# First stage: v of two heads and q, k of a third head in bursts over four k-tiles, summed in SBUF

## The chip, the core and the metric

The kernel runs on one core of one Trainium2 chip. The time is device microseconds of one launch. Engines are named as the profile names them: PE (TensorE matmul; PEld is its weight load), DVE (VectorE), ACT (ScalarE), POOL (GpSimd) and SP (SyncE, which issues most transfers).

## What is computed

One layer of a diffusion backbone (DEPTH is 1): 512 latent tokens and 256 context tokens, 2048 channels, 16 heads of 128, all in f32. A conditioning vector gives shifts, scales and gates by six 2048 x 2048 products (`ada`); then neighbourhood attention with context keys, its output projection, a LayerNorm, a SwiGLU FFN and a second LayerNorm. The part that the change touches is this:

```python
sh1, sc1, g1, sh2, sc2, g2 = [m[:, None, :] for m in ada_params(c, ada_w[i], ada_b[i])]
h = modulate(x, sh1, sc1)                     # x * (1 + sc1) + sh1
hc = modulate(xc, csh1, csc1)
q, k, v = [split_heads(t) for t in jnp.split(h @ w_qkv, 3, axis=-1)]
k_c, v_c = [split_heads(t) for t in jnp.split(hc @ w_qkv[:, D_MODEL:], 2, axis=-1)]
y = neighbourhood_attention(q, k, v, k_c, v_c, na_rpb[j]) @ na_w_o[j]
```

## The kernel before

Every f32 product is made of three `float32r` products (`mm3`: hi x hi, hi x lo, lo x hi). A weight or an activation is first split into hi and lo by `split`: a copy on ACT (line 77) and a subtraction on DVE (line 78). Line 81 is the one matmul call behind nearly all products, so rows are told apart by their tiles.

**First stage.** It walks over 16 k-tiles of 128 channels (`KT`). For k-tile kt, `ada_start` loads four 512 KB pieces of the modulation weights (`wr_an`) and multiplies them with `sil` into bank 7 (`adp`, 32 short matmul rows); `ada_cols` turns the result into the columns `md` of shift and scale; `h_start` loads 128 rows of x (`xr`, 256 KB) and of the context (`cr`, 128 KB) through POOL's queue, modulates them on DVE and splits them into the activations `a_h` and `hc`; `qkv_start` loads a 384 KB piece of `w0` and accumulates q and k of heads 0 and 1 (`acc`, 4 banks), v of both for the latent tokens (2 banks) and their context keys (1 bank). So seven banks are open for the whole stage and the eighth serves `adp`. `ada_start` runs one k-tile ahead of `qkv_start`. All raw pieces come from a ring of six buffers in pool `p0`; `xr` and `cr` share two buffers (`stg`), so the next `xr` is loaded only when the last one has been split.

**Between the stages.** `evac_q` and `split` empty the banks into q, k and v. Then pool `p0` is closed and the pools `pb` and `p1r` are opened in its place: `s_c` (the conditioning vector on all partitions, 1 MB, SiLU on ACT), `mask` and each head's bias table `br` (POOL's queue), and a ring of three raw buffers for weights.

**Attention stage.** `v_block(0, v0, [4, 5])` makes the context v of heads 0 and 1; then for each pair hp, `v_block` makes v of both heads, and `q_block`, `k_block` q and k of each head. The steps of a head's attention (`attn`: four scores with softmax, seven steps of transposition `tr` and product with v into `o`) are queued and interleaved with the blocks of the heads after it (`pop`); what is left is put in front of the next block by `flush`. `ada_more` puts the other modulation columns between the blocks: a load of two 512 KB pieces each (`wr_ada`) and two reductions on DVE (line 141). Each queue and engine works in the order in which a scheduler has written its instructions.

Of the kernel before, what the change touches and what calls it, by code (L numbers as in the profile page):

```python
# [9 lines left out]
F32 = mybir.dt.float32  # L10
F32R = mybir.dt.float32r
AF = mybir.ActivationFunctionType
ALU = mybir.AluOpType
# [4 lines left out]
P = 128  # L18
D = 2048
KT = D // P  # L20
T = 512
C = 256
# [11 lines left out]
U = 1024  # L34
# [9 lines left out]
def build(tc, ins, out):  # L44
    nc = tc.nc
    with ExitStack() as top:
# [5 lines left out]
        def bank(i, name):  # L52
            return psp.tile([P, T], F32, tag=f"b{i}", name=name)
# [11 lines left out]
        act_hi = [None] * KT  # L65
        act_lo = [None] * KT
# [86 lines left out]
        hc_hi = [hcx[k // 2][:, k % 2 * T:k % 2 * T + C] for k in range(KT)]  # L153
        hc_lo = [hcx[k // 2][:, k % 2 * T + C:k % 2 * T + T] for k in range(KT)]

        with ExitStack() as ph1:
            pa = ph1.enter_context(tc.tile_pool(name="pa", bufs=1))
# [4 lines left out]
            def new_q(h):  # L162
                return [pa.tile([P, T], F32R, tag=f"q{i}", name=f"q{h}_{i}", bufs=2) for i in "hl"]

            def new_k(h):
                return [pa.tile([P, T + C], F32R, tag=f"k{i}", name=f"k{h}_{i}", bufs=2) for i in "hl"]

            def new_v(hp):
                return [[pa.tile([P, 2 * P], F32R, tag=f"v{t}{i}", name=f"v{hp}_{t}{i}") for i in "hl"]
                        for t in range(6)]  # L170

            def evac_q(ps, q):
                nc.scalar.activation(q[0], ps, AF.Copy, scale=QSCALE)
                nc.vector.scalar_tensor_tensor(out=q[1], in0=ps, scalar=QSCALE, in1=q[0].bitcast(F32),
                                               op0=ALU.mult, op1=ALU.subtract)

            q0, q1, k0, k1, v0 = new_q(0), new_q(1), new_k(0), new_k(1), new_v(0)

            def half(b, x):
                return b[:, (x % 2) * 256:(x % 2) * 256 + 256]  # L180

            accs = [bank(i, f"acc{i}") for i in range(7)]
            rows, mods = {}, {}

            def ada_start(kt):
# [30 lines left out]
                split(hc_hi[kt], hc_lo[kt], cr[:, :C])  # L216

            def qkv_start(kt):
                wh, wl = unit(ins["w0"][kt], f"w0{kt}", 768)
# [6 lines left out]
                for t in range(4):  # L226
                    ts = slice(t * P, (t + 1) * P)
                    mm3(half(accs[4 + t // 2], t), act_hi[kt][:, ts], act_lo[kt][:, ts],
                        wh[:, 512:768], wl[:, 512:768], f and t % 2 == 0, l)
                for i in (1, 3):  # L230
                    sl = slice(i * P, (i + 1) * P)
                    mm3(half(accs[6], i // 2), wh[:, sl], wl[:, sl], hc_hi[kt], hc_lo[kt], f and i == 1, l)

            with tc.tile_pool(name="p0", bufs=6) as p0:
                rp[0] = p0
                sil = p0.tile([P, KT, 32], F32, name="sil", bufs=1)
                nc.gpsimd.memset(sil, 0.0)
                for i in range(2):
                    nc.vector.tensor_copy(sil[:, :, i], cv[:, i])
                ada_start(0)  # L240
                biases()
                ada_cols(0)
                for kt in range(KT):
                    h_start(kt)
                    if kt + 1 < KT:
                        ada_start(kt + 1)
                    qkv_start(kt)
            for i, (q, k) in enumerate(((q0, k0), (q1, k1))):
                evac_q(accs[2 * i], q)
                split(k[0][:, :T], k[1][:, :T], accs[2 * i + 1])  # L250
                split(k[0][:, T:], k[1][:, T:], half(accs[6], i))
            for t in range(4):
                split(v0[t][0], v0[t][1], half(accs[4 + t // 2], t))
# [169 lines left out]
            for hp in range(1, NH // 2):  # L423
                if hp == 1:
                    enqueue(attn(1, q1, k1, v0), 24)
                v = new_v(hp)
                v_block(hp, v, list(range(6)))
                flush()
                ada_more(3)
                for i in range(2):  # L430
                    h = hp * 2 + i
                    q, k = new_q(h), new_k(h)
                    q_block(h, q)
                    ada_more(1)
                    k_block(h, k)
# [679 lines left out]
def _lay(inp):  # L1115
    a = {k: np.asarray(v) for k, v in inp.items()}
    ct = np.ascontiguousarray
    r = {}
    x = a["x"].reshape(ROWS, NB, BAND, D).transpose(1, 0, 2, 3).reshape(T, D)
    r["xT"] = ct(x.T).reshape(KT, P, T)  # L1120
    r["ctxT"] = ct(a["ctx"].reshape(C, D).T).reshape(KT, P, C)
    r["c"] = ct(a["c"].reshape(D))
    r["cv"] = ct(np.stack([a["c"].reshape(KT, P).T, a["c_ctx"].reshape(KT, P).T], 1))
    aw = a["ada_w"][0]
    r["ada_n"] = ct(aw[:, :2 * D].reshape(KT, P, 2, KT, P).transpose(3, 1, 0, 2, 4)).reshape(KT, P, KT * 2 * P)
    r["ada_t"] = ct(aw[:, 2 * D:].T).reshape(64, P, D)
# [8 lines left out]
    r["w0"] = ct(np.concatenate([w[:, :, 0, 0], w[:, :, 1, 0], w[:, :, 0, 1], w[:, :, 1, 1],  # L1135
                                  w[:, :, 2, 0], w[:, :, 2, 1]], -1))
# [28 lines left out]
```

## Time and profile before

| | us |
|---|---|
| median of 3 runs | 2503.3 (2501.56 to 2512.56) |
| the profiled execution | 2513.77 |
| its span, first to last instruction | 2512.0 |
| PE busy | 2420.1 (96%) |
| DVE busy | 1836.1 (73%) |
| ACT busy | 1038.4 (41%) |
| mean granted TensorE clock | 0.994 |

Busy PE time is modelled: a matmul's row ends later than the next one starts, so work on PE is counted here from start to start. The first stage lies between 0 and 152.6 us of the span, the attention stage from there to about 1000 us.

### The profile page before, as it was taken

How to read it: one execution, taken by the hardware profiler on the slowest of the kernel's cores; microseconds unless marked ns; L12 is line 12 of the kernel's file. 1: busy time of each engine (PE TensorE's matmuls, PEld its weight loads, DVE VectorE, ACT ScalarE, POOL GpSimd, SP SyncE). 2: the span in 40 equal slices, each digit the busy share in tenths (PEclk: the TensorE clock that was granted, in tenths of full speed). 3: DMA queues.
4: the chain of work that ended last, by engine and by line, in shares of the span. 5: the costliest groups of instructions: out<-in, count | busy, mean ns of one | idle time of the engine just before them, and what ended most of it. 6: DMA issues, size and time to landing. Idle time of an engine off the chain costs nothing.

```text
span 2512.0 us, 45142 instructions
## 1 busy us (share of the span) xinstructions
PE 2420.1 (96%) x18588; PEld 2295.4 (91%) x18588; DVE 1836.1 (73%) x2619; ACT 1038.4 (41%) x1590; POOL 234.2 (9%) x348
## 2 busy tenths in 40 slices
PE   7889999999999999999999999999999989999997
PEld 5688989898998988999999999999999979999897
DVE  3365655565565567999888888878888887878978
ACT  2242322222232235548444444444444544645545
POOL 1110101000010000110110100101011000000021
PEclk9999999999999999999999999999999999999999
DMA  9964444444544453655443434433344565754685
GB/s 334 326 231 154 145 162 139 154 155 154 165 154 156 136 187 129 193 121 191 136 133 118 137 124 137 140 120 130 125 144 153 183 196 129 205 158 126 176 185 127
DMA packets 142543, 406.18 MB, mean 162 GB/s; under 512 B 16544, under 2 KB 40496, under 8 KB 142208
## 3 DMA queue, kind: packets, MB, share of 16 engines
q1 hardware_dynamic: 116608, 342.42, 41.5%
q0 software_dynamic: 25728, 60.88, 9.9%
q8 instruction: 145, 2.38, 0.4%
q14 instruction: 62, 0.51, 0.1%
HBM read 351.85 MB, written 40.89 MB: 156 GB/s over the span
## 4 chain that ended last, share of the span: by engine, by line
issue 38%; PE 35%; DMA 11%; DVE 9%; POOL 4%; ACT 2%; SPq 0%; POOLq 0%; ACTq 0%; DVEq 0%
DMA wr_ada<-ada_t 7%; PE qp L81 5%; PE kp L81 4%; PE vp L81 4%; PE cp L81 2%; PE g_1b L81 2%; POOL setT L594 2%; PE y L81 2%; DVE wr_ada L141 2%; PE g_5b L81 1%; PE g_4b L81 1%; PE g_3b L81 1%; PE g_2b L81 1%; PE g_0b L81 1%; POOL setB L594 1%
## 5 line engine op out<-in xcount | busy, mean ns | idle before, releaser
L623 DVE TENSOR_TENSOR wr_f<-wr_f,wr_f 128x1024 f32<-128x1024 f32 x164 | 199.9, 1219 | 3.1 <-DMA wr_f<-w_in 1.7
L81 PE MATMUL vp<-wh_v,a_h 128*128 128x256 f32 x896 | 168.6, 280 | 0.0
L141 DVE CUSTOM_DVE_ANT_0 wr_ada<-wr_ada,s_c,bin 128x1024 f32<-128x1024 f32 x64 | 84.3, 1316 | 87.5 <-DMA wr_ada<-ada_t 87.2
L81 PEld LDWEIGHTS vp<-wh_v,a_h 128*128 128x128 f32 x896 | 141.8, 189 | 0.6
L81 PE MATMUL kp<-a_h,wh_k 128*128 128x512 f32 x448 | 141.2, 396 | 0.0
L81 PE MATMUL qp<-a_h,wh_q 128*128 128x512 f32 x448 | 140.6, 395 | 0.0
L141 DVE CUSTOM_DVE_ANT_0 wr_ada<-wr_ada,s_c,adap 128x1024 f32<-128x1024 f32 x64 | 82.2, 1284 | 78.7 <-DMA wr_ada<-ada_t 78.7
L81 PE MATMUL vp<-wl_v,a_h 128*128 128x256 f32 x448 | 125.5, 280 | 0.0
L623 DVE TENSOR_TENSOR wr_g<-wr_g,wr_g 128x896 f32<-128x896 f32 (+1 forms) x96 | 107.7, 1131 | 7.7 <-DMA wr_g<-w_out 6.7
L77 ACT CAST th<-tr 128x256 fp32r<-128x256 f32 (+2 forms) x96 | 45.8, 477 | 155.2 <-PE tr L318 155.1
L81 PEld LDWEIGHTS cp<-hc,wh_k 128*128 128x128 f32 x448 | 84.1, 188 | 20.3
L594 POOL DMA_DIRECT2D setB<-h x66 | 35.6, 543 | 711.0 <-DVE h L1007 692.6
L81 PE MATMUL vp<-wh_v,hc 128*128 128x256 f32 x512 | 99.8, 283 | 0.0
L81 PEld LDWEIGHTS qp<-a_h,wh_q 128*128 128x128 f32 x448 | 82.1, 188 | 16.5
L301 ACT ACTIVATE p<-sc,sm 128x256 f32<-128x256 f32 x64 | 30.4, 475 | 145.4 <-DVE sm L299 145.2
L81 PE MATMUL cp<-hc,wh_k 128*128 128x256 f32 x448 | 89.5, 281 | 0.0
L81 PE MATMUL qp<-a_h,wl_q 128*128 128x512 f32 x224 | 88.6, 395 | 0.0
L81 PE MATMUL kp<-a_h,wl_k 128*128 128x512 f32 x224 | 88.4, 395 | 0.0
L78 DVE TENSOR_TENSOR tl<-tr,th 128x256 fp32r<-128x256 f32 (+2 forms) x96 | 52.6, 552 | 48.4 <-ACT th L77 48.4
L81 PEld LDWEIGHTS vp<-wl_v,a_h 128*128 128x128 f32 x448 | 84.6, 189 | 0.6
L81 PEld LDWEIGHTS vp<-wh_v,hc 128*128 128x128 f32 x512 | 83.0, 191 | 0.1
L274 POOL TENSOR_TENSOR bv<-br,mask 128x256 f32<-128x256 f32 (+1 forms) x48 | 45.3, 969 | 403.4 <-DVE sm L304 371.5
(1882 smaller groups left out, 8491.1 us busy)
## 6 DMA issues: line engine op xcount, KB each, us to landing
wr_f<-w_in SPq DMA_DIRECT2D x164, 512.0 KB, 4.1
wr_ada<-ada_t SPq DMA_DIRECT2D x128, 512.0 KB, 3.9
wr_an<-ada_n SPq DMA_DIRECT2D x64, 512.0 KB, 6.7
wr_g<-w_out SPq DMA_DIRECT2D x64, 448.0 KB, 4.6
wr_v<-w_v SPq DMA_DIRECT2D x32, 512.0 KB, 4.7
wr_g<-w_out SPq DMA_DIRECT2D x32, 512.0 KB, 4.4
wr_q<-w_qk SPq DMA_DIRECT2D x28, 512.0 KB, 4.4
wr_k<-w_qk SPq DMA_DIRECT2D x28, 512.0 KB, 4.0
```

What stands on the lines that cost most here:

```text
L77: nc.scalar.copy(hi, src)
L78: nc.vector.tensor_tensor(out=lo, in0=src, in1=hi.bitcast(F32), op=ALU.subtract)
L81: nc.tensor.matmul(ps, a, b, start=start, stop=stop, skip_group_check=True)
L141: nc.vector.tensor_tensor_reduce(out=raw, in0=raw, in1=s_c[:, half * U:(half + 1) * U], scale=1.0, scalar=bin2[:, i:i + 1] if half == 0 el ...
L274: nc.gpsimd.tensor_tensor(out=bv[:, off:off + n * P].rearrange("p (d r k) -> p d r k", d=n, r=8), in0=brv[:, d0:d0 + n], in1=mask[:, off:o ...
L301: nc.scalar.activation(p[:, nl:nl + C], sc[:, :C], AF.Exp, bias=sm[:, 2:3], accum_out=sm[:, 3:4])
L594: nc.gpsimd.dma_start(setD[n][q], src)
L623: nc.vector.tensor_tensor(out=self.r[out][:, :n], in0=self.r[a][:, :n], in1=self.r[b][:, :n], op=op)
```

## The change

The 768 columns of a `w0` piece become 512: q and k of heads 0 and 1 stay as they were, in banks 0 to 3 (context keys now in bank 4). v of heads 0 and 1 and q, k and context k of head 2 are made in **bursts**. A block of four k-tiles (the last two blocks have two) gets its weights by two loads, `bv` and `bq` (512 KB or 256 KB each), and five bursts: x = 0, 1 are v of two token tiles each, 2 is q, 3 is k, 4 is the context k. A burst multiplies all k-tiles of its block into one of banks 5 and 6, and the sum goes to the f32 tiles `pt0` to `pt4` in SBUF: by a copy on ACT for the first block, by an addition on DVE after that. The bursts of a block are spread over the k-tiles after it. `evac_q` and `split` then read v of heads 0 and 1 and, after `attn(1)` is queued, q and k of head 2 from these tiles, and the attention stage no longer has `q_block(2)` and `k_block(2)`.

```diff
-            accs = [bank(i, f"acc{i}") for i in range(7)]
+            accs = [bank(i, f"acc{i}") for i in range(5)]
+            pt = [None, None] + [pa.tile([P, n], F32, ...) for i, n in ((2, T), (3, T), (4, C))]
...
+            BLOCKS = ((0, 4), (4, 8), (8, 12), (12, 14), (14, 16))
...
+            def burst(b, x):
+                k0, k1 = BLOCKS[b]
+                n = k1 - k0
+                ps = bank(5 + (5 * b + x) % 2, f"bu{b}_{x}")
+                wh, wl = bw["v" if x < 2 else "q"]
...
+                if b == 0:
+                    nc.scalar.copy(pt[x], ps[:, :w])
+                else:
+                    nc.vector.tensor_tensor(out=pt[x], in0=ps[:, :w], in1=pt[x], op=ALU.add)
...
+                    if last:
+                        burst_load(last[0], "v")
                     qkv_start(kt)
+                    if done:
+                        burst_load(done[0], "q")
+                        bursts.extend((done[0], x) for x in range(5))
+                        left = BLOCKS[done[0] + 1][1] - kt
+                    if bursts:
+                        for _ in range(-(-len(bursts) // left)):
+                            burst(*bursts.pop(0))
+                        left -= 1
...
+                    qk2 = new_q(2), new_k(2)
+                    evac_q(pt[2], qk2[0])
...
-                    q_block(h, q)
+                    q, k = qk2 if h == 2 else (new_q(h), new_k(h))
+                    if h > 2:
+                        q_block(h, q)
```

On PE, near the end of a k-tile of the first stage before (`acc_127` is the bank of the context keys, `adp_799` the modulation of a later k-tile):

```order
L81 MATMUL acc_127<-hc_93,wh_w_750 128x256 x2
L81 MATMUL acc_127<-hc_93,wl_w_751 128x256
L81 MATMUL acc_127<-hc_93,wh_w_750 128x256 x2
L81 MATMUL acc_127<-hc_93,wl_w_751 128x256
L81 MATMUL adp_799<-wr_an_0_800,sil 32x256 x4
```

And in the same place of a k-tile now (`bu_2` is the burst of q):

```order
L81 MATMUL acc_125<-hc_94,wh_w_970 128x256 x2
L81 MATMUL acc_125<-hc_94,wl_w_971 128x256
L81 MATMUL bu_2_996<-a_h,bqh_875 128x512 x2
L81 MATMUL bu_2_996<-a_h,bql_876 128x512
L81 MATMUL bu_2_996<-a_h,bqh_875 128x512 x2
L81 MATMUL bu_2_996<-a_h,bql_876 128x512
L81 MATMUL bu_2_996<-a_h,bqh_875 128x512 x2
L81 MATMUL bu_2_996<-a_h,bql_876 128x512
L81 MATMUL bu_2_996<-a_h,bqh_875 128x512 x2
L81 MATMUL bu_2_996<-a_h,bql_876 128x512
L81 MATMUL adp_1020<-wr_an_0_1021,sil 32x256 x4
```

The bursts stand behind a k-tile's own products and ahead of the modulation of a later one.

On PE at the end of the first stage now, from the last burst on (`sc`, `sl` are scores of head 0):

```order
L81 MATMUL bu_4_1644<-hc_97,bqh_1610 128x256 x2
L81 MATMUL bu_4_1644<-hc_97,bql_1611 128x256
L81 MATMUL sc_0_1702<-k_l,q_h 128x256
L81 MATMUL sc_0_1702<-k_h,q_l 128x256
L81 MATMUL sl_0_1701<-k_h,q_l 128x256
L81 MATMUL sc_1_1738<-k_h,q_h 128x256
```

Before, the products of the context v (`vp`) followed the last `acc` at once; now scores of head 0 come first.

On SP, the loads between the stages before:

```order
L105 DMA wr_w_1339<-w 128x768 [waits DMAHW2_49,DVE_49]
L105 DMA wr_v_0_1408<-w_v 128x1024
L105 DMA wr_v_1_1462<-w_v 128x1024
L105 DMA wr_v_2_1510<-w_v 128x1024 [waits DMAHW3_49]
L258 DMA s_c<-c 128x2048 [waits DMAHW4_49,DMAHW5_49,DMAHW0_49,DMAHW6_49,DVE_49,DMAHW7_49,PE_49,Pool_49]
```

And now:

```order
L105 DMA wr_w_1534<-w 128x512 [waits DMAHW2_49,PE_49]
L243 DMA wr_bq_1608<-w_qk 128x2x256 [waits DMAHW3_49,PE_49]
L318 DMA s_c<-c 128x2048 [waits DMAHW2_49,DMAHW1_49,DMAHW4_49,DMAHW0_49,DMAHW5_49,DVE_49,DMAHW7_49,PE_49,Pool_49]
L105 DMA wr_v_0_1665<-w_v 128x1024
L105 DMA wr_v_1_1719<-w_v 128x1024
L105 DMA wr_v_2_1767<-w_v 128x1024
```

`s_c` has moved ahead of the first three pieces of the context v's weights. The value of PE's semaphore for which `s_c` waits was reached before by the last `adp` product, and is reached now by the last product of the last burst (`bu4_4`), because `s_c` lies where pool `p0` was; `mask`, on POOL's queue, waits for the same value, before and now.

## Rows read from the trace of the kernel before

**Rows 1.** Windows: length; busy PE, PEld, DVE, ACT, POOL; clock, DMA share, GB/s.

```profile
100.00:120.00 20.00, 17.61 (x155) 14.18 (x154) 6.38 (x13) 3.86 (x8) 2.14 (x4) 1.00 0.94 345
160.00:180.00 20.00, 18.98 (x159) 18.73 (x158) 16.50 (x39) 9.51 (x25) 4.23 (x4) 1.00 0.54 172
240.00:260.00 20.00, 20.00 (x110) 17.26 (x110) 10.79 (x23) 4.87 (x9) 0.00 (x0) 1.00 0.48 158
```

**Rows 2.** Timeline of one k-tile: start, us, what, idle before and releaser.

```profile
80.21 1.43 PE L81 MATMUL acc<-a_h,wh_w 128*128 128x512 f32 x5 [1.18 <-ACT wh_w L77]
...
83.48 0.36 PE L81 MATMUL acc<-wh_w,a_h 128*128 128x256 f32 x1
...
84.97 0.40 PE L81 MATMUL acc<-hc,wh_w 128*128 128x256 f32 x2
...
85.76 1.93 PE L81 MATMUL adp<-wr_an,sil 128*32 128x256 f32 x32
85.97 0.55 DVE L209 TENSOR_SCALAR xr<-xr,md 128x512 f32<-128x512 f32 x1 [2.08 <-DMA xr<-xT]
...
87.20 0.69 DVE L78 TENSOR_TENSOR a_h<-xr,a_h 128x512 fp32r<-128x512 f32 x1 [0.26 <-ACT a_h L77]
...
88.19 0.54 POOL L208 DMA_DIRECT2D xr<-xT  x1 [8.54 <-DVE a_h L78]
...
88.27 1.43 PE L81 MATMUL acc<-a_h,wh_w 128*128 128x512 f32 x5 [0.57 <-ACT wh_w L77]
```

**Rows 3.** Waits of the first stage: us in total, times, longest.

```profile
DVE xr L209 <- DMA xr<-xT: 31.2, 14, 3.1
```

**Rows 4.** Timeline: the fifth k-tile's first product, and the context v's first.

```profile
52.36 1.43 PE L81 MATMUL acc<-a_h,wh_w 128*128 128x512 f32 x5 [0.85 <-ACT wh_w L77]
...
152.62 0.28 PE L81 MATMUL vp<-wh_v,hc 128*128 128x256 f32 x1
```

**Rows 5.** The chain that ended last: start, us, what; head 2's q and k.

```profile
223.85 11.20 PE qp L81 x48
235.05 0.70 PE kp L81 x3
236.11 0.70 PE kp L81 x3
```

**Rows 6.** Timeline of DVE: k of a head taken from its bank.

```profile
150.59 0.68 DVE L78 TENSOR_TENSOR k_l<-acc,k_h 128x512 fp32r<-128x512 f32 x1
```

**Rows 7.** Timeline of POOL between the stages.

```profile
144.28 0.54 POOL L261 DMA_DIRECT2D mask<-mask  x1 [1.71 <-DMA wr_v<-w_v]
144.81 0.65 POOL L270 DMA_DIRECT2D br<-rpbr  x1
155.00 2.43 POOL L274 TENSOR_TENSOR bv<-br,mask 128x384 f32<-128x384 f32 x3 [9.55 <-DMA br<-rpbr]
```

**Rows 8.** Timeline of ACT between the stages.

```profile
153.64 1.92 ACT L259 ACTIVATE s_c<-s_c 128x2048 f32<-128x2048 f32 x1 [2.28 <-DMA wr_v<-w_v]
...
156.24 1.07 ACT L77 CAST wh_v<-wr_v 128x1024 fp32r<-128x1024 f32 x1
```

**Rows 9.** Timeline of PE between the stages.

```profile
159.28 0.39 PE L81 MATMUL sc<-k_h,q_h 128*128 128x256 f32 x1 [2.29 <-DVE v_1l L78]
...
169.58 0.38 PE L318 MATMUL tr<-ident,p 128*128 128x128 f32 x2
```

**Rows 10.** The tile s_c: its one load, from issue to landing.

```profile
DMA to landing us min/median/max: 9.6/9.6/9.6
```

**Rows 11.** The tile br: its 16 loads, from issue to landing.

```profile
DMA to landing us min/median/max: 3.3/4.1/10.0
```

**Rows 12.** Timeline of PE: a wait in head 0's attention.

```profile
191.64 0.39 PE L81 MATMUL o<-tl,v_3h 128*128 128x256 f32 x1 [2.66 <-DVE tl L78]
```

**Rows 13.** Windows soon after rows 12 (columns as rows 1; the clock is third last).

```profile
194.00:196.00 2.00, 2.00 (x13) 2.00 (x12) 0.72 (x2) 0.00 (x0) 0.00 (x0) 0.57 0.42 166
```

**Rows 14.** Timeline of DVE: an ada reduction that waits for its load.

```profile
189.96 1.28 DVE L141 CUSTOM_DVE_ANT_0 wr_ada<-wr_ada,s_c,adap 128x1024 f32<-128x1024 f32 x1 [2.08 <-DMA wr_ada<-ada_t]
```

More of the change, by code (lines that the diff above doesn't have):

```diff
@@ L180, in half @@
                 return b[:, (x % 2) * 256:(x % 2) * 256 + 256]
-            accs = [bank(i, f"acc{i}") for i in range(7)]
+            accs = [bank(i, f"acc{i}") for i in range(5)]
+            pt = [None, None] + [pa.tile([P, n], F32, tag=f"pt{i}", name=f"pt{i}") for i, n in ((2, T), (3, T), (4, C))]
             rows, mods = {}, {}
@@ L218, in qkv_start @@
             def qkv_start(kt):
-                wh, wl = unit(ins["w0"][kt], f"w0{kt}", 768)
+                wh, wl = unit(ins["w0"][kt], f"w0{kt}", 512)
                 f, l = kt == 0, kt == KT - 1
@@ L225, in qkv_start @@
                     ada_cols(kt + 1)
[L226 to L229, printed above, removed]
                 for i in (1, 3):
                     sl = slice(i * P, (i + 1) * P)
-                    mm3(half(accs[6], i // 2), wh[:, sl], wl[:, sl], hc_hi[kt], hc_lo[kt], f and i == 1, l)
+                    mm3(half(accs[4], i // 2), wh[:, sl], wl[:, sl], hc_hi[kt], hc_lo[kt], f and i == 1, l)
@@ new lines, in build, with burst_load @@
+            BLOCKS = ((0, 4), (4, 8), (8, 12), (12, 14), (14, 16))
+            bw = {}
+            bursts = []
+            def burst_load(b, x):
+                k0, k1 = BLOCKS[b]
+                n = (k1 - k0) * 256
+                raw = raw_tile(f"b{x}{b}")
+                if x == "v":
+                    nc.sync.dma_start(raw[:, :n], ins["w_v"][0, :, k0 * 256:k1 * 256])
+                else:
+                    nc.sync.dma_start(raw[:, :n].rearrange("p (q c) -> p q c", q=2),
+                                      ins["w_qk"][:, 2, :, k0 * P:k1 * P].rearrange("q p c -> p q c"))
+                bw[x] = [p0.tile([P, U], F32R, tag=f"b{x}{i}", name=f"b{x}{i}{b}", bufs=1) for i in "hl"]
+                split(bw[x][0][:, :n], bw[x][1][:, :n], raw[:, :n])
@@ new lines, in burst @@
+            def burst(b, x):
+                k0, k1 = BLOCKS[b]
+                n = k1 - k0
+                ps = bank(5 + (5 * b + x) % 2, f"bu{b}_{x}")
+                wh, wl = bw["v" if x < 2 else "q"]
+                for i in range(2 if x < 2 else 1):
+                    ts = slice((2 * x + i) * P, (2 * x + i + 1) * P)
+                    for kk in range(n):
+                        f, l = kk == 0 and i == 0, kk == n - 1
+                        if x < 2:
+                            s_ = slice(kk * 256, kk * 256 + 256)
+                            mm3(half(ps, i), act_hi[k0 + kk][:, ts], act_lo[k0 + kk][:, ts], wh[:, s_], wl[:, s_], f, l)
+                            continue
+                        o = (x > 2) * n * P + kk * P
+                        s_ = slice(o, o + P)
+                        if x < 4:
+                            mm3(ps, wh[:, s_], wl[:, s_], act_hi[k0 + kk], act_lo[k0 + kk], f, l)
+                        else:
+                            mm3(ps[:, :C], wh[:, s_], wl[:, s_], hc_hi[k0 + kk], hc_lo[k0 + kk], f, l)
+                w = C if x == 4 else T
+                if b == 0:
+                    nc.scalar.copy(pt[x], ps[:, :w])
+                else:
+                    nc.vector.tensor_tensor(out=pt[x], in0=ps[:, :w], in1=pt[x], op=ALU.add)
@@ L239, in build @@
                     nc.vector.tensor_copy(sil[:, :, i], cv[:, i])
+                for x in range(2):
+                    pt[x] = p0.tile([P, T], F32, tag=f"pt{x}", name=f"pt{x}", bufs=1)
                 ada_start(0)
@@ L246, in build @@
                         ada_start(kt + 1)
+                    last = [b for b, (k0, k1) in enumerate(BLOCKS) if k1 == kt + 1]
+                    done = [b for b, (k0, k1) in enumerate(BLOCKS) if k1 == kt]
+                    if last:
+                        burst_load(last[0], "v")
                     qkv_start(kt)
[L248 to L253, printed above, removed]
+                    if done:
[6 more added lines that the diff above has]
+                        left -= 1
+                end = len(BLOCKS) - 1
+                for x in range(2):
+                    burst(end, x)
+                for i, (q, k) in enumerate(((q0, k0), (q1, k1))):
+                    evac_q(accs[2 * i], q)
+                    split(k[0][:, :T], k[1][:, :T], accs[2 * i + 1])
+                    split(k[0][:, T:], k[1][:, T:], half(accs[4], i))
+                    if i == 0:
+                        burst_load(end, "q")
+                for t in range(4):
+                    split(v0[t][0], v0[t][1], half(pt[t // 2], t))
+                for x in range(2, 5):
+                    burst(end, x)
             pb = ph1.enter_context(tc.tile_pool(name="pb", bufs=1))
@@ L425, in build @@
                     enqueue(attn(1, q1, k1, v0), 24)
+                    qk2 = new_q(2), new_k(2)
+                    evac_q(pt[2], qk2[0])
+                    split(qk2[1][0][:, :T], qk2[1][1][:, :T], pt[3])
+                    split(qk2[1][0][:, T:], qk2[1][1][:, T:], pt[4])
                 v = new_v(hp)
@@ L431, in build @@
                     h = hp * 2 + i
-                    q, k = new_q(h), new_k(h)
-                    q_block(h, q)
+                    q, k = qk2 if h == 2 else (new_q(h), new_k(h))
+                    if h > 2:
+                        q_block(h, q)
                     ada_more(1)
-                    k_block(h, k)
+                    if h > 2:
+                        k_block(h, k)
                     ada_more(2)
```

3 lines of the change are left out of this document (1 added, 2 removed).

## The prediction

> **What bounds the kernel now.** I read the page's first section, then stretches of the span, then one k-tile of the first stage, the step between the stages, and the chain where the removed blocks stand.
>
> PE is busy 96% of the span, but not everywhere for the same reason. Between 240 and 260 us, in the attention stage, it is busy throughout while the DMA engines are half used; between 100 and 120 us, in the first stage, the DMA engines are at 0.94 and PE has gaps [rows 1]. Why, one k-tile tells [rows 2]. PE spends 3.27 us on q and k and the modulation's columns (80.21 to 83.48), 1.49 on v, 0.79 on the context keys, 1.93 on `adp`: 7.5 us. Then it waits for the next weights, whose split stands on ACT behind the split of `xr`. `xr` itself came late: DVE waited 2.08 us for it, and in the stage it waits so 14 times, 31.2 us in all [rows 3]. The loop is closed by the buffers: `xr` lands, is modulated and split (85.97 to 87.89), and only then the next `xr` is issued, at 88.19 [rows 2]. Nearly all of a k-tile's time is thus a loaded DMA queue. From the fifth k-tile's first product to the stage's end 100.3 us pass [rows 4]; PE's own work in them is 10 x 7.5 for k-tiles 4 to 13, 5.6 for 14 and 5.0 for 15 (no `adp`), 85.6 us. PE has some 15 us free there, and about 4 more in the first four k-tiles.
>
> **What leaves the attention stage.** q of head 2 is 48 products in 11.20 us, 0.233 each; three of k and three of the context k take 1.06 us, so 16 k-tiles take 17.0 [rows 5]. That is 28.2 us on a PE that is never idle there. The steps of `attn(1)` are flushed before these blocks and those of `attn(2)` are queued behind them, so nothing else is hidden under them on PE. All 28.2 us count.
>
> **What the first stage gets.** A product of 256 columns is (1.06 - 0.70) / 3 = 0.12 us. Per block of four k-tiles v is 48 of them, 5.8 us, q and k 2.8 each, the context k 1.4: 12.8 us; the two short blocks are 6.4 each. A k-tile's base is 7.5 - 1.49 = 6.0 us. The first block's bursts start in the fifth k-tile (kt 4). From its first product to the end of kt 15's own products PE has: base 10 x 6.0, 4.1 for kt 14 and 3.5 for kt 15, 67.6; bursts of blocks 0 to 2, 38.4, and 4.3 of block 3 (both v and q, in kt 14). Sum 110.3 us.
>
> - Start: kt 0 to 2 carry 128 KB less each, of 2.75 MB, so their 8.5 us shrink by some 0.4; the fifth k-tile starts at 51.5 instead of 52.36.
> - Stalls: kt 4 and 8 hold 11.8 us of PE work and kt 12 14.6, so their loads are ready ahead; kt 7 and 11 hold 7.4, less than the 8.06 between two k-tiles in rows 2, and there the loop shows again. I take 1.2 us for each of these two and 0.1 for the rest, 3 us (bounds: none, and 7 if every k-tile keeps half the present gap).
> - DMA: bursts of v bring as many bytes as they take out of `w0`; q and k are 2.1 MB more in the stage, 0.13 MB a k-tile on 2.9. At the 345 GB/s of rows 1 a k-tile's bytes then need 8.7 us, under PE's 9.2. No term of its own.
> - DVE and ACT: 20 additions of at most 0.68 us [rows 6] and the same splits as before in other pieces. DVE has 13 of 20 us free [rows 1]. An addition waits for its burst, and behind it on DVE stand the low half of the next weights and `xr`'s modulation; PE's cover for that is `adp`, 1.93 us, against two additions and a split of 512 columns, 2.0. Nothing while `adp` runs; 0.1 us where it doesn't.
>
> So kt 15's own products end at 51.5 + 110.3 + 3 = 164.8, before at 152.62 [rows 4]. Behind them come the rest of block 3 (2.1 us) and all of block 4 (6.4), with some 0.3 of waits for additions to empty banks 5 and 6: the last burst ends at 173.6.
>
> **The step between the stages.** Here the change adds a wait. Before, three pieces of the context v's weights were loaded early, and `s_c`, `mask` and `br` were issued at 144 us, so that 8 us of products still lay over them. Now `s_c` on SP and `mask` on POOL wait for the last burst's last product, since they lie in its pool's place; on SP all weights of the attention stage are queued behind `s_c`, on POOL `br` behind `mask`. On PE some scores of head 0 are ready (1.2 us); then it waits for two chains. Bias: issue of `mask` and `br` 1.2 us, landing, the first of three additions on POOL (a third of 2.43 us) [rows 7], some 0.5 us of DVE for the first softmax step. Weights: landing of `s_c`, its SiLU 1.92 us, then the cast of the first piece, 1.07 us, behind it on ACT [rows 8]. Landing: 9.6 us for `s_c` [rows 10] and 10.0 for a `br` in a full queue, 4.1 for one in a quiet one [rows 11]. With 9.6 to 10.0 PE starts again some 12.8 us after the last burst; with 4.1 for `br` and 5.5 for the larger `s_c`, 8.8. I take 11.0, near the loaded rows: `s_c`, three weight pieces, `mask` and `br`, 3.3 MB, leave together.
>
> The Trainium skill ("DMA: Bandwidth & Descriptors", section "Queues, rings and completion order") says that each DMA engine takes turns between the queues that have work. By that `mask` and `br` need only wait for their own bytes and as many of SP's, about 1.3 MB or 4 us at 345 GB/s, an estimate, and the sum would be 3 us lower. Rows 7 and 10 show no such preference: POOL's small loads landed no sooner than `s_c`.
>
> From there to head 0's first transposition: before, 152.62 to 169.58, 17.0 us, of which PE waited 2.29 [rows 9]; less that and the 1.2 us of scores already made, 13.5. So it starts at 173.6 + 11.0 + 13.5 = 198.1, 28.5 us later than before.
>
> **Clock.** After the wait of 2.66 us at 191.64 [rows 12] the granted clock was 0.57 for a while [rows 13], mostly the lower of its two levels (1.2 of 2.4 GHz); some 4 us at that level cost 2 us more. After the wait of 2.29 us at 159.28 the clock stayed at 1.00 [rows 1, 9]. I take 1.5 us for the new gap (0 to 2.5). The Trainium skill ("TensorE: Matmul & The Clock Gate", section "What's actually happening") says that half rate is the resting state and work releases it; by that the full 2 us belong in the sum. Of the two waits one agrees.
>
> **DVE behind it.** Without head 2's blocks twelve `ada` reductions instead of six stand on SP and DVE ahead of head 3's q, among the softmax steps of heads 0 and 1. Each is 1.28 us and may wait 2.08 for its load [rows 14], with PE behind it. PE has v products between the steps; I take 1.5 us (0 to 5).
>
> **Sum.** -28.2 + 28.5 + 1.5 + 1.5 = +3.3 us. The rest of PE's order, from head 3's q on, is as before. The profiled execution took 2513.77, 10 above the median of 2503.3 and just above the slowest run shown, so I carry the difference over to the median: 2506.
>
> **Rivals.**
>
> - The new wait closes early: `br` and `s_c` land like lone loads, PE restarts after 8 us, without a drop of the clock. 3 + 1.5 lower, and half of the stalls gone: -4 to -9, 2496. For it: nothing else is in the queue then. Against: 3.3 MB at 345 GB/s are 9.5 us.
> - The bursts fit better than counted: no stalls (-3), the gap at 7 us (-4), no clock drop, and the 2.66 us of rows 12 with its slow products, which hang on the same DVE steps, not met again (-5): 2490 or less. That is faster by over 0.5%. Against: PE's free time of 19 us is less than the 28 it is to take in.
> - Slower: the step between the stages as the bound. `s_c` blocks SP, so not one but all four pieces of the context v's weights come late, and each next piece must pass ACT and DVE among the first softmax steps, which now run at the same time. If each of the three later pieces costs 3 us and the restart takes 13, that is +11 on the sum, 2517 to 2520. It decides when the last burst and head 0's first transposition are more than 34 us apart; I count 24.5.
> - The change does not do what it says where the stage stays bound by DMA: then it lasts as long as before plus 2.1 MB, 6 us, and the bursts cost little; with the same step behind it that is about the early case, 2496. Counted there.
>
> **How the numbers follow.** Forecast 0.62 (2506, from 2498 to 2514); early 0.14; fits 0.10; slower 0.14. Measurement of this kernel tells about 0.5%, 12.5 us, from no change: below 2490.8 is faster, 0.10; above 2515.8 is slower, 0.14; the forecast and the early case are the same, 0.76. The range leaves out the fitting case and half of the slower one: 2494 to 2519.
>
> **What would show it.** The fifth k-tile's first product near 51.5; periods of 9 to 12 us from there, 14 to 15 in kt 12; the last burst's end near 173.6; a PE gap of 8 to 12 us behind it, ended by `wh_v` or a softmax step, with `s_c` and `mask` issued at its start; the first transposition near 198; head 3's q right behind head 1's last step, about where head 3's q stood before (252 us). Wrong would be a gap under 6 us, a last burst before 165 us (the stage had more room than I counted) or after 180, or PE waits for `ada` loads between the gap and head 3's q that sum to over 5 us.

## The result, and the profile after

| | before | after |
|---|---|---|
| median, us | 2502.4 (2498.3 to 2512.6) | 2530.9 (2524.0 to 2538.9) |
| ratio to before, same chip | | 1.0092 [1.0072, 1.0112] |
| span of the profiled execution | 2512.0 | 2528.7 |
| mean granted clock | 0.994 | 0.988 |

The change makes the kernel slower by 0.9%, about 23 us (18 to 28). The two medians alone would say 1.011; the ratio compares runs of one chip, and a repeat (below) gave 1.0085. I had forecast +3 and no measurable difference.

Four marks tell where; behind the last, head 4's first `qp` product, all kernels do the same work in the same order.

| us of the span | before | forecast | after |
|---|---|---|---|
| last product of the first stage | 152.8 | 173.6 | 185.4 |
| first transposition of head 0 | 169.6 | 198.1 | 216.0 |
| head 3's q | 252.0 | 255.3 (252.0 + 3.3) | 272.6 |
| head 4's q | 333.3 | | 353.0 |

So 11.8 us too much were lost in the first stage, 6.1 in the step behind it, and little after that. The first stage first. The timeline of after in its k-tile 8, of POOL, ACT, DVE and PE (columns: start, length, engine, line, operation, names, then idle time before it and what ended it; rows between are left out):

```profile
89.53 0.54 POOL L209 DMA_DIRECT2D xr<-xT  x1 [8.86 <-DVE a_h L78]
...
91.95 0.62 ACT L77 CAST wh_w<-wr_w 128x512 fp32r<-128x512 f32 x1
...
92.82 0.16 DVE L203 TENSOR_TENSOR md<-adp,bin 128x4 f32<-128x4 f32 x1 [3.25 <-PE adp L81]
...
93.26 1.09 PE L81 MATMUL acc<-a_h,wh_w 128*128 128x512 f32 x4
96.47 0.55 DVE L210 TENSOR_SCALAR xr<-xr,md 128x512 f32<-128x512 f32 x1 [3.48 <-DMA xr<-xT]
96.93 0.68 DVE L78 TENSOR_TENSOR wl_w<-wr_w,wh_w 128x512 fp32r<-128x512 f32 x1
...
97.67 1.22 PE L81 MATMUL acc<-a_h,wl_w 128*128 128x512 f32 x2 [3.32 <-DVE wl_w L78]
```

The low half `wl_w` of k-tile 8's weights could have been made at 92.6, when its cast was done. DVE is in the way: in its order the modulation of `xr` of k-tile 9 stands ahead of `wl_w` of k-tile 8, and that `xr`, issued at 89.53, lands only at 96.4. PE has four products that need the high half alone, then it stands for 3.32 us. In k-tile 12 the same happens:

```profile
140.93 0.73 PE L81 MATMUL acc<-a_h,wl_w 128*128 128x512 f32 x2 [2.90 <-DVE wl_w L78]
```

In before, `wl_w` of a k-tile stands ahead of the next `xr` on DVE in every k-tile. Now it stands behind it in k-tiles 1 to 4 and in 8 and 12, where bursts begin: the scheduler has turned them. DVE's waits between 50 and 170 us, grouped (total, times, longest):

```profile
DVE md L203 <- PE adp L81: 38.7, 11, 6.7
DVE pt L271 <- PE bu L81: 13.1, 7, 3.3
...
DVE xr L210 <- DMA xr<-xT: 6.6, 2, 3.5
```

DVE now waits mostly for PE, and in this stretch for `xr` only twice; in the trace of [rows 3] 11 of the 14 such waits lie behind 50 us. The DMA engines have room in parts of the stage, 0.66 between 100 and 120 us against 0.94 in [rows 1], but not where these two waits arise:

```profile
89.50:96.50 7.00, 4.85 (x48) 3.12 (x40) 0.26 (x3) 0.89 (x2) 1.07 (x2) 1.00 0.91 306
132.00:140.00 8.00, 5.92 (x56) 3.56 (x54) 1.58 (x5) 0.96 (x3) 1.07 (x2) 1.00 0.94 321
100.00:120.00 20.00, 20.00 (x159) 15.87 (x157) 6.41 (x12) 2.91 (x6) 2.05 (x4) 0.97 0.66 228
```

These two `xr` took 6.8 and 6.9 us from issue to landing, the others from k-tile 6 on 2.9 to 4.5. Around the first of them, issued at 89.53, SP issues the second load of the block's weights (`wr_bq`, 84.92), which before does not have, and four pieces of `wr_an` (from 89.64); that these delay it is read from the order of the issues and was not tested.

Now the step behind the stage; its last burst product started at 185.16. The loads, the chain to the first softmax step, and PE:

```profile
185.52 0.33 SPq L318 DMA_DIRECT2D s_c<-c  x1
...
186.01 0.54 POOL L321 DMA_DIRECT2D mask<-mask  x1 [24.80 <-DVE pt L271]
186.54 0.64 POOL L330 DMA_DIRECT2D br<-rpbr  x1
190.21 1.91 ACT L319 ACTIVATE s_c<-s_c 128x2048 f32<-128x2048 f32 x1 [6.88 <-DMA s_c<-c]
193.62 1.04 ACT L77 CAST wh_v<-wr_v 128x1024 fp32r<-128x1024 f32 x1 [1.50 <-DMA wr_v<-w_v]
...
195.97 2.40 POOL L334 TENSOR_TENSOR bv<-br,mask 128x384 f32<-128x384 f32 x3 [8.79 <-DMA br<-rpbr]
...
197.64 1.25 PE L81 MATMUL sl<-k_h,q_h 128*128 128x256 f32 x2 [10.87 <-DVE sm L356]
201.73 0.58 PE L81 MATMUL vp<-wl_v,hc 128*128 128x256 f32 x1 [1.56 <-DVE wl_v L78]
```

That is the wait I had named, and nearly its size: 12.4 us from last burst to restart, 11.0 forecast. What I had too small is the clock behind it. Stretches of 2 us (busy time of PE, PEld, DVE, ACT, POOL, then PE's granted clock, DMA share, GB/s):

```profile
188.00:190.00 2.00, 0.00 (x0) 0.00 (x0) 0.00 (x0) 0.00 (x0) 0.00 (x0) 0.95 0.99 369
190.00:192.00 2.00, 0.00 (x0) 0.00 (x0) 0.00 (x0) 1.79 (x1) 0.00 (x0) 0.50 0.90 307
...
204.00:206.00 2.00, 2.00 (x12) 2.00 (x11) 1.03 (x2) 0.00 (x0) 1.71 (x2) 0.50 0.57 170
206.00:208.00 2.00, 2.00 (x15) 2.00 (x15) 0.48 (x3) 0.97 (x1) 0.59 (x1) 0.79 0.70 256
```

PE works from 197.64 to some 207 at the lower level (1.2 GHz), busy for 7.8 us of that, which costs half of it, 3.9 us, instead of 1.5.

### The profile page after: what moved, and what is told of

It reads as the page before. It is cut to its first block, busy times and chain, and to the rows that moved or that the text cites. A ratio compares the mean times of both kernels' runs of the same rounds, so it can differ in the third digit from the quotient of the medians.

```text
span 2528.7 us, 45205 instructions
## 1 busy us (share of the span) xinstructions
PE 2435.7 (96%) x18588; PEld 2304.7 (91%) x18588; DVE 1847.7 (73%) x2645; ACT 1044.0 (41%) x1601; POOL 236.5 (9%) x348
## 4 chain that ended last, share of the span: by engine, by line
issue 38%; PE 35%; DMA 11%; DVE 10%; POOL 4%; ACT 2%; POOLq 0%; SPq 0%; DVEq 0%; ACTq 0%
DMA wr_ada<-ada_t 7%; PE qp L81 5%; PE kp L81 4%; PE vp L81 4%; PE cp L81 2%; PE g_1b L81 2%; POOL setT L660 2%; DVE wr_ada L141 2%; PE y L81 2%; PE g_3b L81 1%; PE g_5b L81 1%; PE g_4b L81 1%; PE g_2b L81 1%; POOL setB L660 1%; PE g_0b L81 1%
## 5 line engine op out<-in xcount | busy, mean ns | idle before, releaser
L81 PE MATMUL kp<-a_h,wh_k 128*128 128x512 f32 x416 | 131.3, 397 | 0.0
L81 PE MATMUL qp<-a_h,wh_q 128*128 128x512 f32 x416 | 130.6, 395 | 0.0
L81 PEld LDWEIGHTS cp<-hc,wh_k 128*128 128x128 f32 x416 | 78.2, 188 | 18.8
L81 PEld LDWEIGHTS qp<-a_h,wh_q 128*128 128x128 f32 x416 | 76.1, 188 | 15.1
L81 PE MATMUL cp<-hc,wh_k 128*128 128x256 f32 x416 | 83.1, 281 | 0.0
L81 PE MATMUL qp<-a_h,wl_q 128*128 128x512 f32 x208 | 82.3, 396 | 0.0
L81 PE MATMUL kp<-a_h,wl_k 128*128 128x512 f32 x208 | 82.1, 395 | 0.0
```

Of the source, the lines that this page charges most:

```text
L81: nc.tensor.matmul(ps, a, b, start=start, stop=stop, skip_group_check=True)
```

## Experiments

All ratios are to the kernel before on the same chip; on the chips of these runs the median of before was 2514 to 2517 us, so times of different chips are not compared. "q4" is head 4's q in the profile (before: 333.3, and 334.9 in a second trace). `after_(a, b)` is an edge that only fixes the order of two instructions on their engine.

**The order on DVE alone.**

```diff
+                if kt in (5, 9, 13):
+                    after_(last_lo[0], xm)   # wl_w of kt - 1, then xr of kt
```

> The changed kernel; only the order on DVE in k-tiles 4, 8 and 12 is turned: wl_w of the k-tile stands ahead of the next k-tile's xr instead of behind it. Theory A (the fixed order on DVE makes PE wait for an xr that it does not need yet): the PE gaps of 3.3 us near 98 and 2.9 us near 141 go, and with them most of the 4 us at half clock behind each (some 2 us of time each); the last burst ends near 177 instead of 185.3, the whole is 7 to 10 us shorter than the changed kernel, about 2522. Rival B (xr itself lands too late, whoever waits for it): the wait moves to the products with the next a_h; gain under 2 us. Rival C (the stage simply holds more PE work than I counted): no change of the last burst's end.

Measured: 1.0061 [1.0041, 1.0080], 8 us under the change's 1.0092. The two gaps are gone:

```profile
97.14 0.69 DVE L78 TENSOR_TENSOR wl_w<-wr_w,wh_w 128x512 fp32r<-128x512 f32 x1
...
97.47 0.86 PE L81 MATMUL acc<-a_h,wh_w 128*128 128x512 f32 x3
...
100.68 0.55 DVE L217 TENSOR_SCALAR xr<-xr,md 128x512 f32<-128x512 f32 x1 [2.85 <-DMA xr<-xT]
```

`xr` still comes late (DVE waits 2.85 us for it), and PE no longer waits behind it. From the cast of k-tile 4's weights to the last burst's end 124.2 us pass (56.80 to 181.04), in after 131.2 (54.23 to 185.44). By the forecast's own count, which gives 122.1 from the first product, 0.9 behind the cast, it would be 123. So theory A holds; B and C are out. The last burst ended at 181, not 177: in k-tiles 1 to 3, which the edit leaves alone, this trace lost 6.26 us to the same order.

**`xr` early, DVE's order as in the change.**

```diff
-                return pa.tile([P, T], F32, tag="stg", name=name, bufs=2)
+                return pa.tile([P, T], F32, tag="stg", name=name, bufs=4)
```

> The changed kernel with four stage buffers instead of two, so that xr and cr are loaded one k-tile earlier; DVE's order is as in the changed kernel, wl_w of k-tiles 4, 8 and 12 still behind the next xr. Theory A (a late xr together with that order makes the waits): the PE gaps of 3.3 and 2.9 us with wl_w as releaser go; from k-tile 4's weights to the last burst's end 122 to 126 us instead of 131; 6 to 10 us under the changed kernel in the first stage. Rival (DVE is simply too slow with the splits and additions, whatever xr does): the waits stay, under another name, and the stage is within 2 us of the changed kernel's.

Measured: 1.0027 [1.0014, 1.0040], 16 us under the change, by a change of one number. In its k-tile 8:

```profile
90.51 0.55 DVE L210 TENSOR_SCALAR xr<-xr,md 128x512 f32<-128x512 f32 x1
...
90.75 1.09 PE L81 MATMUL acc<-a_h,wh_w 128*128 128x512 f32 x4
90.97 0.68 DVE L78 TENSOR_TENSOR wl_w<-wr_w,wh_w 128x512 fp32r<-128x512 f32 x1
...
91.71 0.73 PE L81 MATMUL acc<-a_h,wl_w 128*128 128x512 f32 x2
```

The wait for `xr` has left DVE's list, no PE gap of 0.9 us or more is left in the stage from 25 us on, and 120.5 us pass from k-tile 4's cast to the last burst's end (51.68 to 172.15). All 20 additions and all splits of the bursts are still there: DVE is not too slow; it was held up by the wait at its head.

**The same in the kernel before.** The same line, in before.

> The kernel before with four stage buffers instead of two. If the old stage was held by the loop of xr's buffer (landing, modulation, split, next issue), it shortens by 4 to 9 us, since the DMA engines were at 0.94 of their time. If it was held by the DMA engines themselves, it is within 3 us of the kernel before.

Measured: 1.0005 [0.9988, 1.0023]. The second reading: `xr`'s buffer, which I had called the loop that closes the old stage, was not its bound; that the DMA engines were (0.94 in [rows 1]) is what is left, and was not tested by itself. The 31.2 us of [rows 3] cost nothing that shows.

**The loads of the step, early.**

```diff
+                mask = pa.tile([P, 896], F32, name="mask")   # and br0: own places,
+                dm = nc.gpsimd.dma_start(mask, ins["mask"])  # issued in k-tile 13
...
+                early = [unit(ins["w_v"][0, :, u * U:(u + 1) * U], f"v0_{u}") for u in range(2)]
                 for x in range(2, 5):
                     burst(end, x)
...
             v_block(0, v0, [4, 5])
+            s_c = pb.tile([P, D], F32, name="s_c")           # was ahead of it
```

> The changed kernel; mask and head 0's br are loaded in k-tile 13 into places of their own, the first two pieces of the context v's weights are loaded and split ahead of the last bursts, and s_c is loaded behind the context v's weights. Theory A (the step between the stages waits for loads that the last burst holds back): the PE gap of 10.9 us behind the last burst falls under 3 us, the half clock from 189 to 207 goes; head 0's first transposition stands 18 to 22 us behind the last burst instead of 30.7, and the whole is 10 to 15 us shorter than the changed kernel, about 2518. Rival B (the softmax of head 0 on DVE and ACT is what takes the time there, with the splits of v0 and of head 2 beside it): the gap goes but the first transposition still stands 27 us or more behind the last burst; gain under 4 us.

Measured: 1.0060 [1.0037, 1.0083], 8 us under the change. The stage ends where it did in after (185.6), there is no PE gap of 0.3 us behind it up to 202.8 (the first is 1.32, at 204.19), and the clock stays up:

```profile
190.00:192.00 2.00, 2.00 (x19) 2.00 (x17) 1.54 (x7) 1.99 (x6) 0.00 (x0) 1.00 1.03 428
```

Head 0's first transposition stands 11.2 us behind the last burst, and head 3's q starts 71.4 us behind it instead of 87.2. In the trace that is 16 us, in the ratios 8, give or take as much: single traces scatter by some 5 us behind this place too.

**Both edits.** The two diffs above (order and loads) together.

> Both edits together: wl_w ahead of the next xr in k-tiles 4, 8, 12, and mask, br and the first weights loaded early. If they are two separate losses, the gains add: 17 to 25 us under the changed kernel, about 2510, within 0.5% of the kernel before. If the second stage only waits for something later (softmax steps, the ada loads behind them), the sum is no better than the larger of the two.

Measured: 1.0020 [1.0005, 1.0035], 18 us under the change, q4 335.3. The gains add, as far as the intervals tell (8 and 8 alone, each give or take some 7).

**Only v in bursts.**

```diff
-                        burst_load(done[0], "q")
-                        bursts.extend((done[0], x) for x in range(5))
+                        bursts.extend((done[0], x) for x in range(2))
...
+                    q_block(h, q)      # head 2's q and k back in the attention stage
```

> Half of the change: v of heads 0 and 1 in bursts as in the changed kernel, but head 2's q and k stay in the attention stage, so no PE work moves. Theory A (the loss is waits, at the step between the stages above all): the first stage ends about as in the kernel before, some 3 us later for the last v burst, and the step behind it costs its gap of 11 us and 4 us of half clock: 13 to 20 us over the kernel before, about 2519. Rival C (the loss is the PE work of head 2 that does not fit into the first stage): without it the kernel is within 4 us of the kernel before.

Measured: 1.0138 [1.0119, 1.0157], 35 us over before: worse than the whole change, and by more than theory A said. No work of head 2 is in the stage, yet its last burst ends at 175.9. In k-tile 8:

```profile
88.84 0.55 DVE L210 TENSOR_SCALAR xr<-xr,md 128x512 f32<-128x512 f32 x1 [4.66 <-DMA xr<-xT]
...
90.87 0.68 DVE L78 TENSOR_TENSOR wl_w<-wr_w,wh_w 128x512 fp32r<-128x512 f32 x1
...
91.61 1.65 PE L81 MATMUL acc<-a_h,wl_w 128*128 128x512 f32 x3 [5.18 <-DVE wl_w L78]
```

It is the same wait, and longer, for PE has less to do beside it; and DVE's order is turned in more places, k-tiles 1 to 4, 7, 8, 11, 12 and 14. Rival C falls: without head 2's work in the stage the loss is larger, not gone.

**Neither, and the moved term by itself.** Two kernels in which head 2 works on head 1's q and k. One is before without `q_block(2)` and `k_block(2)`, the other after without the q and k bursts.

```diff
-                    q, k = new_q(h), new_k(h)
-                    q_block(h, q)
+                    q, k = (q1, k1) if h == 2 else (new_q(h), new_k(h))
+                    if h > 2:
+                        q_block(h, q)
```

> The kernel before without head 2's q and k blocks and their loads: head 2 works on head 1's q and k, the rest is as before. This is the term of -28.2 us by itself, together with what the ada reductions do that then stand in a row on DVE. By the prediction -28.2 + 1.5 (0 to 5): 25 to 28 us under the kernel before. Rival: the blocks hid waits of the attention steps of heads 0 and 1 or of the ada loads; then the gain is under 20 us.

> The changed kernel without head 2's q and k altogether (neither in bursts nor in blocks; head 2 works on head 1's): only v in bursts and the step behind it are left. Beside the kernel before without its blocks (0.9944) it prices v in bursts and the step alone; beside the changed kernel it prices the q and k bursts, 28 us of PE work, in the first stage. Theory A (waits decide): it lies 30 us or more above the kernel before without blocks, that is within 10 us of the changed kernel: the q and k bursts cost little where they stand. Rival C (they cost their PE work): it is 20 us or more under the changed kernel.

Measured: 0.9944 [0.9922, 0.9965], 14 us (9 to 20), where I had 25 to 28; by the ratio that is the rival's case. In the trace q4 stands at 313.5, 20 to 21 us earlier. And 1.0071 [1.0052, 1.0090] for v in bursts alone, 32 us over the other one. So the q and k bursts, 28 us of PE work, cost 4 to 5 us of the whole time (1.0085 and 1.0092 against 1.0071, whose intervals overlap), although the stage ends 10 to 15 us later with them than without (175.2): they fill waits. Theory A.

Part of what the first kernel is short of shows in its trace, at the end of head 1's steps:

```profile
227.98 1.28 DVE L141 CUSTOM_DVE_ANT_0 wr_ada<-wr_ada,s_c,adap 128x1024 f32<-128x1024 f32 x1 [3.52 <-DMA wr_ada<-ada_t]
229.19 0.42 DVE L78 TENSOR_TENSOR tl<-tr,th 128x256 fp32r<-128x256 f32 x1
...
229.66 0.39 PE L81 MATMUL o<-tl,v_3h 128*128 128x256 f32 x1 [2.70 <-DVE tl L78]
```

and at the same place in the second trace of before:

```profile
224.53 1.28 DVE L141 CUSTOM_DVE_ANT_0 wr_ada<-wr_ada,s_c,adap 128x1024 f32<-128x1024 f32 x1 [2.05 <-DMA wr_ada<-ada_t]
...
226.22 0.39 PE L81 MATMUL o<-tl,v_3h 128*128 128x256 f32 x1 [0.54 <-DVE tl L78]
```

The last softmax tile `tl` waits behind an `ada` reduction that waits for its load; with more reductions in a row the wait grew from 0.54 to 2.70, and some 4 us at the lower clock followed it, 2 us lost. After has it too (2.40 us at 272.26). That is the seam I had put at 1.5 us (0 to 5). It makes some 4 us of the 5 that the trace is short of; for the further 7 of the ratio, 14 us instead of 21, I have no row, and the cause stays open.

**PE kept busy in the step's gap.**

```diff
+                    if h == 0 and j == 2:
+                        for i in range(36):
+                            mm(keep, act_hi[0][:, :P], act_hi[i % 16], i == 0, i == 35)
```

> The changed kernel with 36 products that nobody reads (512 columns, some 8 us at full clock) in the PE gap behind the last burst; they wait for nothing, and the scores of queries' blocks 2 and 3 stand behind them. The gap's waits are unchanged, so this prices the half clock from 189 to 207 us alone. If the clock falls because PE waits, it now stays at 1.00 there, and head 0's first transposition comes 3 to 5 us earlier. If it falls for another reason, the products run at half clock, take up to 16 us, and the step gets some 5 us longer.

Measured: 1.0110 [1.0081, 1.0140], no gain. The products ran at full clock, but 30 of them are 6.96 us, and the weights came later than that:

```profile
194.56 6.96 PE L83 MATMUL keep<-a_h 128*128 128x512 f32 x30
204.36 0.58 PE L83 MATMUL vp<-wh_v,hc 128*128 128x256 f32 x1 [2.84 <-ACT wh_v L77]
```

```profile
202.00:204.00 2.00, 0.00 (x0) 0.00 (x0) 0.00 (x0) 0.74 (x1) 0.00 (x0) 1.00 1.02 291
204.00:206.00 2.00, 1.64 (x4) 1.38 (x5) 0.00 (x0) 1.59 (x2) 0.76 (x1) 0.59 0.40 148
...
212.00:214.00 2.00, 2.00 (x12) 2.00 (x11) 0.96 (x1) 0.00 (x0) 0.00 (x0) 0.50 0.88 266
```

The clock held until the wait of 2.84 us and then fell for some 10 us, as after the long gap. So here a gap of 2.84 us was as dear, in clock, as the one of 10.87, and the price of the clock alone was not measured. From the last burst's end to the first transposition 31.3 us passed, in the two traces of after 30.5 and 30.8.

**Both kernels again.** No edit.

> The kernel before once more, for a trace on the same chip as the runs beside it. The first trace (span 2512.0) lay 10 us above the median of its own runs. If that was scatter in one place, this one shows where: the first stage's end (152.8 us there), head 3's q (252.0), the rest behind it (2260 us).

> The changed kernel once more, on the same chip as the runs beside it: ratio 1.007 to 1.011 as before. The trace shows which of its parts repeat: the PE gaps with wl_w as releaser in k-tiles 8 and 12, the gap of 10 to 12 us behind the last burst, half clock for some 10 us behind that; and whether the fifth k-tile's late start (55.5 us) repeats or is scatter (51.6 to 57 in the runs with the same order up to there).

Measured: 1.0002 [0.9987, 1.0016] and 1.0085 [1.0057, 1.0114]. The traces give two warnings. The first trace of before had a short first stage and a long rest: here the stage ends at 157.3 instead of 152.8, head 4's q is at 334.9, and yet the span is 2504.9 instead of 2512.0. And the turned order costs in the first k-tiles as well: here, as in three other runs with bursts, `xr` of k-tile 2 was late, and `wl_w` of k-tile 1 stood behind it:

```profile
31.61 0.55 DVE L210 TENSOR_SCALAR xr<-xr,md 128x512 f32<-128x512 f32 x1 [5.76 <-DMA xr<-xT]
...
32.81 1.22 PE L81 MATMUL acc<-a_h,wl_w 128*128 128x512 f32 x2 [5.89 <-DVE wl_w L78]
```

The gaps of k-tiles 8 and 12 (3.99 and 3.09 us) and the one behind the last burst (11.05) repeat.

**A second buffer and early loads, `cr` and `br` cut short.** Here `cr` got one small buffer of its own, and `br` stayed late.

```diff
+                cr = pa.tile([P, C], F32, tag="cr", name=f"cr{kt}")
...
+                mask = pa.tile([P, 896], F32, name="mask")
```

> The changed kernel with a second buffer for xr (cr gets a smaller one of its own), mask loaded in k-tile 13 into a place of its own, the first two pieces of the context v's weights loaded and split ahead of the last bursts, and s_c behind them; br stays where it was. If the two losses are what I say, the first stage's last burst ends near 172 and head 3's q starts near 245: 22 to 28 us under the changed kernel, 0 to 10 us under the kernel before. If head 0's br, which still waits for the last burst, holds the step (PE gap over 4 us there), or if the time is given back behind head 3's q, it is no better than the kernel with both edits, 1.002.

Measured: 1.0050 [1.0035, 1.0066], worse than the second buffer alone (1.0027). Both shortcuts cost a wait, each by the same mechanism:

```profile
46.21 0.41 DVE L224 TENSOR_SCALAR cr<-cr,md 128x256 f32<-128x256 f32 x1 [3.17 <-DMA cr<-ctxT]
...
47.67 0.68 DVE L78 TENSOR_TENSOR wl_w<-wr_w,wh_w 128x512 fp32r<-128x512 f32 x1
...
48.41 0.97 PE L81 MATMUL acc<-a_h,wl_w 128*128 128x512 f32 x3 [3.49 <-DVE wl_w L78]
...
196.92 0.58 PE L81 MATMUL vp<-wl_v,hc 128*128 128x256 f32 x1 [6.45 <-DVE wl_v L78]
```

Now `cr` is the late one that `wl_w` stands behind, and `wl_v` stands behind the softmax steps that wait for `br`.

**The same with room for all.** Four stage buffers, of which three take head 0's mask (in two halves) and `br` when the last k-tiles are done with them; the context v's first two pieces early.

```diff
+                mA, mB, br0 = stage("mA"), stage("mB"), stage("br0")
+                nc.gpsimd.dma_start(mA[:, :384], ins["mask"][:, :384])
+                nc.gpsimd.dma_start(mB, ins["mask"][:, 384:])
```

> The changed kernel with both cures, this time without the side effects that the last try showed (cr's single buffer held POOL's queue up, and br still came after the last burst): four stage buffers, two of which take head 0's mask as two halves and a third br once xr and cr of the last k-tiles are done with; the first two pieces of the context v's weights ahead of the last bursts; s_c and the mask of the later heads behind them. If the two losses are separate and are all of it: last burst near 172, PE gaps behind it under 2 us each, head 4's q near 326 (before: 333.3 and 334.9), ratio 0.994 to 0.999. If q and k of head 2 in bursts have a cost of their own that the waits only hid, it stays at 1.002 or more.

Measured: 1.0003 [0.9991, 1.0015]: the loss is gone, and nothing is won. q4 is at 337.8. The last burst ends at 179.8, with 1 us of context v products (9 of 0.12) already between the bursts, and the first gap of over 0.85 us behind it is 1.68 at 195.90. It lies between the two cases that I had named: without the two waits the kernel is level with before, and the gain I had expected did not come. The stage is late by itself here, for from k-tile 4's cast to the last burst's end 126.5 us pass (1 of them for context v), against 120.5 with the four buffers alone. Most of that is at k-tile 15: PE waits 1.47 us for `a_h` and 0.84 for an addition, and the clock is at 0.50 behind it.

## Why the prediction was wrong

**What moved.** The count of PE's work in the stage held. The kernel that comes nearest to the forecast's terms is the one with `xr` early, which keeps the step's gap: its last burst ends at 172.15 (forecast 173.6), and it takes 1.0027, 7 us over before (4 to 10). With its stage 1.5 us under the forecast and its step 5.7 over (30.2 from the last burst's end to the first transposition, for 24.5) the sum of 3.3 would be 7.5. So there the -28.2 is borne out to some 3 us. The kernel without the blocks does not: 14 us (9 to 20) for 26.7, of which rows explain some 4. And that the last kernel comes out near the forecast's 2506 is luck: it has neither the gap of 11.0 nor the 1.5 of clock, which the sum contains, and pays 6 us in its stage instead (179.8 for 173.6).

**The step that failed: the items on DVE and on stalls.** I had summed what DVE has to do in a k-tile (2.0 us of it ahead of the next weights) against what covers it (1.93 us of `adp`) and put the difference, 0.1 us, in the sum; and I had taken 3 us of stalls (0 to 7) from the old loop, for k-tiles 7 and 11, with the loads of 4, 8 and 12 "ready ahead". Both treat DVE as an amount of work. It is a queue, and the change altered its order in k-tiles 1 to 4, 8 and 12: `wl_w` behind an `xr` that PE needs only a k-tile later. The waits came in 8 and 12. Measured, the stage ran 11.8 us over the forecast, past the 180 that I had named as a sign of being wrong. From k-tile 4's cast on the forecast's steps come to 123, of which 1.4 us (12 products of the first burst, 0.12 each) already stand ahead of that cast in the trace: 9.6 us were lost there, 3.32 + 2.90 of waits, and half clock behind each from 98 to 101 and from 142 to 145, some 1.6 us each. The other 2 lie ahead of that cast, where the clock was down from 43 to 50:

```profile
44.00:46.00 2.00, 1.70 (x5) 1.29 (x5) 1.24 (x3) 1.09 (x3) 0.00 (x0) 0.50 1.02 410
```

The fifth k-tile's later start, 55.5 for 51.5, holds these and 17 products of the first burst (2.0 us), which I had counted behind it; and my 51.5 rested on a trace of before that was early (k-tile 4's cast at 51.5; 53.8 in its second trace). With the order mended in k-tiles 4, 8 and 12 the stage takes 124.2 us from that cast, with `xr` early 120.5, and the forecast's steps come to 121.6: the count of PE's work was right to 3 us. The order of DVE's instructions is fixed in the program and could be read beforehand; I had read it at the step between the stages only. The Trainium skill ("DVE: scalar operands, raw-bit mode, write accounting and state across instructions", section "Flops that outlive an instruction") says in passing that DVE's queue is one in-order queue; the trace agrees, with 3.48 us of waiting at 96.47 in front of a split whose inputs were ready.

**xr's buffer.** I called the stage's bound "a loaded DMA queue" closed by that buffer. A second buffer gives before nothing and after 16 us. The 31.2 us of [rows 3] belong to one trace: the second trace of before has three such waits, 3.4 us in all, and its stage is no shorter (157.3). What made the wait dear in after is who stands behind it on DVE; mending that order alone left `xr` late and took the two gaps away. I had also spread the bytes of q and k evenly, 0.13 MB a k-tile. Over the stage the DMA engines are at 0.67 in after and 0.92 in before, but where the two waits arise they are at 0.91 and 0.94.

**The step between the stages.** The mechanism was right, and so was the size of the gap, 12.4 for 11.0. From restart to the first transposition 18.3 us passed for my 13.5 and 1.5: 3.9 of clock, and 1.56 for `wl_v`, which I had not counted. I had given a landing in 4 us some chance; `s_c` landed in 4.5, but `br`, issued last, took 9.3, and the bias chain hangs on `br`:

```profile
mask<-mask POOLq DMA_DIRECT2D x1, 448.0 KB, 7.3
br<-rpbr POOLq DMA_DIRECT2D x1, 192.0 KB, 9.3
```

**My slower rival** had the right place but not the price: it was to decide at 34 us between last burst and first transposition. It was 30.7, and the kernel was slower still, because the stage before it was late as well. The two are separate, each worth some 8 to 16 us alone, and no case of mine had both.

**The clock** was counted for one gap. There are five falls in after's first 280 us (43 to 50, 98 to 102, 142 to 146, 190 to 207 and 237 to 241) and two in before; the second traces have six and three.

**ada behind it**: 1.5 us (0 to 5) forecast; from first transposition to head 3's q 56.6 us for 54.2. Right in size, and shown by the row of the kernel without blocks.

## What to carry to other kernels

When work is moved into a stage that waits for something, list what each in-order engine now has queued, k-tile by k-tile, and look for an instruction that waits for a transfer ahead of one that the critical engine needs next; sums of busy time don't show it. A wait that costs nothing behind one order of instructions (here 31 us of it in one trace) can cost behind another: see who stands behind it, and free its buffer first. And where a pool's release holds loads back, move the loads out before counting on the time behind it.

## What was not expected of the hardware

How long PE waits did not by itself tell whether the clock falls. At one and the same product, in two executions of the changed kernel, it stayed at 1.00 through and behind a wait of 2.40 us, and stood at 0.50 behind one of 2.44 (the first trace of after, then its second):

```profile
272.26 0.39 PE L81 MATMUL o<-tl,v_3h 128*128 128x256 f32 x1 [2.40 <-DVE tl L78]
274.00:276.00 2.00, 2.00 (x13) 1.73 (x12) 1.94 (x4) 0.38 (x2) 0.36 (x1) 1.00 0.62 240
...
277.14 0.58 PE L81 MATMUL o<-tl,v_3h 128*128 128x256 f32 x1 [2.44 <-DVE tl L78]
278.00:280.00 2.00, 2.00 (x6) 1.52 (x6) 2.00 (x4) 1.45 (x3) 0.57 (x1) 0.50 0.73 240
```

In the last kernel it fell behind waits of 1.68 and 0.61 us, one close behind the other (195.90 and 196.95). The Trainium skill ("TensorE: Matmul & The Clock Gate", section "What's actually happening") says that the hardware judges PE's activity on a clock of its own that does not start with the kernel's work; these places do not contradict it, and no run here tests it. For a forecast it means that a gap of some 2 us may cost 2 us more, or nothing.
